# Passing from layer 1 to layer 2 one stream at a time, and new places for dense fill

## The chip, the core and the metric

One core of a Trainium2 chip. The kernel is one launch, and its time is the device time of that launch in microseconds (us). Five engines run their own instruction streams: PE (TensorE, the matmuls), DVE (VectorE), ACT (ScalarE), POOL (GpSimd) and SP (SyncE, which here only issues DMAs). A tile's data passes from one to the next by semaphores.

## What is computed

Two layers of a hybrid block over 256 latent tokens `x` and 256 context tokens `ctx`, width 1024. The reference, cut to the layer:

```python
for l in range(DEPTH):                       # DEPTH = 2
    mod_x = silu(c) @ w_mod[l] + b_mod[l]    # shift, scale, gate; the same for ctx with c_ctx
    hx  = rmsnorm(x,  g_pre[l]) * (1 + sc_x) + sh_x
    hcn = rmsnorm(hc, g_pre[l]) * (1 + sc_c) + sh_c
    # zx = hx @ w_in, zc = hcn @ w_in: cut into the three branches' inputs, their gates, merge gates
    o_rw, o_na, o_df = rwkv7_both_directions(z), neighbourhood_attention(z), differential_attention(z)
    yb = einsum('btnc,ncd->btnd', o * silu(g), w_branch)      # one 512 -> 1024 product a branch
    y  = sum(sigmoid(mg) * yb) @ w_out
    x  = x  + gt_x * rmsnorm(y_x, g_post[l])
    hc = hc + gt_c * rmsnorm(y_c, g_post[l])                  # not in the last layer
return x
```

The last layer needs the context only as keys, values and RWKV states, so its gates, merge and output product run for the 256 latent tokens alone.

## The kernel before

**Dense products.** Each float32 product is made of three products of rounded operands (`mm3`, L244: high·high, high·low, low·high). A weight comes in chunks of 128 × 512 (256 KB, `chunk`, L217, DMA issued by SP into a ring of 6 buffers `wr`); ACT rounds it to `wh` (ring of 5) and DVE subtracts to get the low part `wl` (ring of 4) (`split`, L226). The layer's input stands transposed in 16 tiles `self.h` (8 high, 8 low, features on the partitions, 512 tokens wide: columns 0 to 255 are x, 256 to 511 are ctx). `z_pair` (L270) makes 256 output features of it in four chunks.

**Order of the work.** The program is written as generators. The RWKV branch (`rwkv`: groups of scores, a triangular inverse `rwkv_inv` L777, state steps `rwkv_steps` L837, all in two segments) and then attention (`attn`, L1034) are the main strings. They yield numbers from the table `self.yl` (one row a layer), and `weave` (L1437) puts so much dense work (`fill`) between their pieces. Fill is, in this order, the projections and gates that the branches still need (`zs`, L1367: gates, `rwkv_z`, `mgates`, `attn_z`), beside it the gate part of the modulation (`mods`, L1361), and then the merge of branch 0 and 1. A bigger number in the table takes fill from later places, a smaller one leaves it to them; fill that is used up can't cover a wait. A list scheduler then settles each engine's order; each engine executes strictly in order.

**The passage.** After the third branch's merge, `merged` (L1261) adds and rounds the eight merged tiles `s`. `outproj` (L1269) multiplies all 512 tokens by `w_out`: 4 column groups `c` of 256, each of 4 chunks `kh`; a chunk serves 4 token tiles, so 24 matmuls of 256 columns. ACT squares and DVE multiplies by the gate row as each `c` ends. Then come, for all four token tiles at once, `residual` (L1299: reduce, `rsqrt` L201, 8 multiply-adds) and `start` (L449): `norm_rows`, the transposition of the rows by PE (`turn_rows`, 32 transposes of 128 × 128), the modulation by DVE and ACT and the split into `self.h`. The shift and scale of layer 2 (`mod_rows`, L362: 4 groups of 32 matmuls on 32 columns) run here too: the weights come during `outproj`, two of the groups run after its last matmul. Then follow r (chunk 0, x alone), the low-rank inputs (chunk 6), k and v.

**Tail.** In layer 2 `outproj` serves x's two token tiles, and `residual` writes the result.

The instruction helpers stand at L164 (ACT), L185 (tensor_tensor), L189 (tensor_scalar), L192 (scalar_tensor_tensor), L195 (matmul), L199 (transpose), L179 (reduce). In names, `k` is any general tile, `a`, `z`, `y`, `b` are PSUM tiles.

## Time and profile before

| | |
|---|---|
| median of 3 runs | 1435.5 us (1427.74 to 1436.76) |
| the profiled execution's own time | 1432.81 us |
| its span | 1430.8 us |
| mean granted clock of TensorE, share of full speed | 0.96 |
| PE busy | 1316.2 us (92%) |
| weight loads (PEld, beside PE) | 1099.1 us (77%) |
| DVE busy | 973.6 us (68%) |
| ACT busy | 812.4 us (57%) |
| POOL busy | 234.8 us (16%) |

So PE is the engine that sets the time, and 114.6 us of the span pass without a matmul. The stretches of the kernel, by the names on PE in the timeline: layer 1 up to 771.4 us, the passage 771.4 to 888.9, layer 2's first RWKV half to about 1134, its second inverse 1134.5 to 1193.4, second steps 1193.4 to 1236.8, attention 1252.5 to 1349, merges and output to the end.

### The profile page before, as it was taken

Reading aid. Unit: us, or ns where it says so; the run is one execution under the profiler, and the core shown is the slowest. Engines: PE = TensorE matmul, PEld = TensorE weight load, DVE = VectorE, ACT = ScalarE, POOL = GpSimd, SP = SyncE. Lnnn points to the kernel's source line nnn. Section 1 sums busy time; section 2 is a strip of 40 time slices with the busy share of each in tenths; the row PEclk is TensorE's granted clock in tenths of the full one; section 3 lists DMA queues with packets and bytes.
Section 4 is the critical chain, followed back from the end, with each engine's and each line's share of the span. In section 5 each row is a group of like instructions: output and inputs, shape, how many; then the busy total and the mean of one; then the engine's idle time right before and its main releaser. Section 6 shows DMA issues by size and latency. Waiting matters only on the chain. (4 is left out here: it accounts for less than half of the span.)

```text
span 1430.8 us, 28581 instructions
## 1 busy us (share of the span) xinstructions
PE 1316.2 (92%) x10784; PEld 1099.1 (77%) x10784; DVE 973.6 (68%) x2047; ACT 812.4 (57%) x1750; POOL 234.8 (16%) x292
## 2 busy tenths in 40 slices
PE   6999999999998999999899969998999998989796
PEld 4865877789777876677778948887888788967686
DVE  4763579626887367768675357768747892689886
ACT  5462375535864436667533356766549736477653
POOL 0010011002110011223245001011111000032441
PEclk9999999899998899999999989999989998999999
DMA  9366632414323268422643843553613242685454
GB/s 357 125 205 201 201 123 89 126 61 148 119 67 118 69 168 243 142 97 82 201 144 118 303 159 103 185 170 121 182 61 97 75 140 69 180 272 171 131 168 148
DMA packets 112986, 212.42 MB, mean 148 GB/s; under 512 B 13088, under 2 KB 24880, under 8 KB 112848
## 3 DMA queue, kind: packets, MB, share of 16 engines
q1 hardware_dynamic: 102896, 178.33, 39.3%
q0 software_dynamic: 9952, 32.26, 6.9%
q8 instruction: 85, 1.39, 0.4%
q14 instruction: 53, 0.43, 0.1%
HBM read 176.70 MB, written 33.83 MB: 147 GB/s over the span
## 5 line engine op out<-in xcount | busy, mean ns | idle before, releaser
L195 PE MATMUL z<-k,wh 128*128 128x512 f32 (+1 forms) x2288 | 631.7, 359 | 8.6 <-ACT wh L164 4.5
L195 PEld LDWEIGHTS z<-k,wh 128*128 128x128 f32 x2288 | 404.8, 193 | 75.1 <-issue 9.7
L195 PE MATMUL z<-k,wl 128*128 128x512 f32 (+1 forms) x1144 | 407.5, 358 | 8.5 <-DVE wl L185 8.5
L164 ACT ACTIVATE wh<-wr 128x512 fp32r<-128x512 f32 x376 | 234.0, 630 | 295.8 <-PE z L195 172.3
L185 DVE TENSOR_TENSOR wl<-wr,wh 128x512 fp32r<-128x512 f32 x376 | 280.3, 752 | 168.0 <-PE z L195 66.8
L195 PEld LDWEIGHTS z<-k,wl 128*128 128x128 f32 x1144 | 220.5, 193 | 41.5 <-DVE wl L185 13.0
L195 PE MATMUL z<-wh,k 128*128 128x256 f32 x704 | 142.1, 296 | 1.5 <-ACT k L164 1.3
L195 PEld LDWEIGHTS z<-wh,k 128*128 128x128 f32 x704 | 117.4, 201 | 3.4 <-ACT k L164 1.5
L185 POOL TENSOR_TENSOR k<-k,k 64x512 fp32r<-64x512 f32 (+3 forms) x64 | 78.4, 1231 | 165.9 <-ACT k L164 88.3
L195 PE MATMUL z<-wl,k 128*128 128x256 f32 x352 | 103.9, 295 | 1.7 <-DVE wl L185 1.5
L164 ACT ACTIVATE gs<-z 128x512 f32<-128x512 f32 (+1 forms) x132 | 66.2, 502 | 61.7 <-PE z L195 52.6
L164 ACT ACTIVATE k<-k 64x256 fp32r<-64x256 f32 (+5 forms) x154 | 79.2, 541 | 29.4 <-POOL k L185 21.6
L185 DVE TENSOR_TENSOR k<-k,k 128x256 f32<-128x256 f32 (+5 forms) x126 | 79.5, 644 | 17.5 <-ACT k L164 14.3
L199 PE MATMUL b<-cst,k 128*128 128x128 f32 x384 | 67.4, 292 | 20.7 <-ACT k L164 5.5
L199 PEld LDWEIGHTS b<-cst,k 128*128 128x128 f32 x384 | 45.3, 147 | 42.0 <-issue 13.6
L164 ACT ACTIVATE k<-a,s 128x512 f32<-128x512 f32 (+1 forms) x96 | 59.2, 617 | 32.1 <-DVE s L179 31.3
L164 ACT ACTIVATE k<-b 128x256 f32<-128x256 f32 (+1 forms) x152 | 67.4, 472 | 16.7 <-PE b L199 15.9
L195 PEld LDWEIGHTS z<-wl,k 128*128 128x128 f32 x352 | 70.8, 201 | 2.9 <-DVE wl L185 2.3
L195 PE MATMUL a<-k,k 128*128 128x512 f32 (+1 forms) x192 | 61.2, 400 | 12.1 <-ACT k L164 9.9
L195 PE MATMUL a<-ar,bk 64*128 64x128 f32 (+1 forms) x512 | 50.0, 285 | 9.8 <-ACT Lab L164 9.0
L195 PEld LDWEIGHTS a<-ar,bk 64*128 64x128 f32 x512 | 42.4, 187 | 21.5 <-ACT Lab L164 16.3
L179 DVE TENSOR_REDUCE s<-a 128x1 f32<-128x512 f32 (+1 forms) x96 | 56.4, 587 | 1.7 <-PE a L195 1.7
(169 smaller groups left out, 1952.4 us busy)
## 6 DMA issues: line engine op xcount, KB each, us to landing
wr<-in_wi SPq DMA_DIRECT2D x296, 256.0 KB, 3.0
k<-in_wm SPq DMA_DIRECT2D x64, 256.0 KB, 5.7
wr<-in_wb SPq DMA_DIRECT2D x48, 256.0 KB, 2.6
md<-gs SPq DMA_DIRECT2D x36, 256.0 KB, 2.8
k<-md POOLq DMA_DIRECT2D x36, 256.0 KB, 4.5
wr<-in_wg SPq DMA_DIRECT2D x32, 256.0 KB, 3.0
wr<-in_wo SPq DMA_DIRECT2D x32, 256.0 KB, 4.8
gd<-gs SPq DMA_DIRECT2D x18, 256.0 KB, 3.0
```

Of the source, the lines that this page charges most:

```text
L164: return self.nc.scalar.activation(out=out, in_=in_, func=func, **kw)
L179: return self.nc.vector.tensor_reduce(out=out, in_=in_, axis=AX.X, op=op, **kw)
L185: return (eng or self.nc.vector).tensor_tensor(out=out, in0=a, in1=b, op=op)
L195: return self.nc.tensor.matmul(out, lhsT=lhsT, rhs=rhs, start=start, stop=stop)
L199: return self.nc.tensor.transpose(out, in_, self.ident[0:k, 0:k])
```

## The change

1. `outproj` works on one stream, x first, then ctx, so `w_out` is read and split twice (16 chunks more). In the last column group the first token tile's four chunks run before the second tile's, and `done` (residual, `norm_row`) of the first tile follows at once. `stream_in` transposes, modulates and splits one stream, 256 columns wide. `start_next` then makes r and the RWKV gates of x, before chunks 6, 2 and 4, which need both streams.
2. While ctx's output product, r and these gates run, the low parts of the weights are made by POOL instead of DVE (`lo_eng`): 16 + 4 + 8 chunks.
3. The shift and scale of layer 2 (`mod_next`) are made in layer 1 as fill, one group after a piece of gates, through the ring `wr`.
4. The RWKV gates of layer 2 thereby leave its fill.
5. The table `yl` has new numbers, and `rwkv_inv` has two more places that take fill (`q`).
6. `rsqrt` for one column has 8 operations instead of 10. `residual` works by token tile, in the tail too. Two general slots fewer (50).

```diff
-        self.yl = [dict(inv=(59.8, 32.75), qq=(6, 9.66), step=(6, 6), na=(2.5, 1.19), diff=(0.8, 2.9), nd=(2, 5), A=(0, 0), B=(0, 4), G=(0.75, 0), C=(5.6, 7.2)),
-                   dict(inv=(25.5, 54), qq=(3.0, 0), step=(6, 6), na=(1.0, 2.3), diff=(4.69, 8.12), nd=(0, 2), A=(0, 0), B=(4.5, 0), G=(0, 0), C=(4.0, 6.0))]
+        self.lo_eng = None
+        self.yl = [dict(inv=(57, 30), qq=(6, 9.66), step=(6, 6), na=(2.5, 1.19), diff=(0.8, 2.9), q=(1.0, 1.0), nd=(2, 5), A=(0, 0), B=(0, 4), G=(0.75, 0), C=(5.6, 7.2)),
+                   dict(inv=(11.0, 51), qq=(4.5, 0), step=(6, 6), na=(1.0, 2.3), diff=(5.86, 8.12), q=(0, 1.0), nd=(3.0, 3.5), A=(0, 3.0), B=(4.5, 0), G=(0, 0), C=(0, 6.0))]
...
+        if n == 1:
+            a, y, t = (self.small(1) for _ in range(3))
+            self.ts(a, v, scale, eps, ALU.mult, op)
...
+            self.tt(y, t, y, ALU.mult)
+            return y
...
-        self.tt(lo, w, h.bitcast(F32), ALU.subtract)
+        self.tt(lo, w, h.bitcast(F32), ALU.subtract, self.lo_eng)
...
+    def mod_next(self, l, P):
+        rows = self.stage(512)
+        self.dma(self.nc.gpsimd, rows, self.io["rows"][l, :, 0:512])
+        A, B, gp = self.mod_tiles(l, P)
+        for g in range(4):
+            mp = self.ps("z", (128, 128))
+            for k in range(8):
+                w = self.chunk(self.io["wm"][l, g, k])
+                for i in range(4):
+                    self.mm(mp[32 * i:32 * i + 32, :], self.cs[:, k].rearrange("p a b -> p (a b)"),
+                            w[:, 128 * i:128 * i + 128], k == 0, k == 7)
+            self.mod_cols(A, B, gp, mp, rows[:, 128 * g:128 * g + 128], g)
+            yield 3.2
+            for _ in range(3):
+                yield 0
...
+    def stream_in(self, P, hn, s):
+        c = slice(256 * s, 256 * s + 256)
+        for k in range(8):
+            p = self.ps("b", (128, 256))
+            self.turn_rows(hn, k, p)
+            t = self.slot((128, 256))
+            A, B = P["A"][:, s, k:k + 1], P["B"][:, s, k:k + 1]
+            self.ts(t, p, A, B, ALU.mult, ALU.add)
+            self.act(self.h[0][k][:, c], p, AF.Identity, scale=A, bias=B)
+            self.tt(self.h[1][k][:, c], t, self.h[0][k][:, c].bitcast(F32), ALU.subtract)
+    def norm_row(self, x):
+        ss = self.small(2)
+        for j in range(2):
+            self.act(self.stage(512), x[j], AF.Square, accum_out=ss[:, j:j + 1])
+        s2 = self.small(1)
+        self.red(s2, ss, ALU.add)
+        rs = self.rsqrt(s2, 1, 1.0 / 1024, RMS_EPS)
+        self.act(x[0], x[0], AF.Copy, scale=rs)
+        self.ts(x[1], x[1], rs)
+    def start_next(self, l, P, nr):
+        self.lo_eng = self.nc.gpsimd
+        r = self.now(self.z_pair(l, 0, 0, nr))
+        self.rwkv_rows(l, P, 0, 1, r, 0, nr, False)
+        self.now(self.gates(l, nr, 0))
+        self.lo_eng = None
+        self.rwkv_wa(l, P, self.now(self.z_pair(l, 6, 0, T)), 0, T)
+        row = [self.rwkv_rows(l, P, 0, w, self.now(self.z_pair(l, c, 0, T)), 0, T, True) for w, c in ((0, 2), (2, 4))]
+        self.have["rx", l, 0] = True
+        self.have["rz", l, 0] = row[0], [None, None], row[1]
...
             Qs.append(q)
+            yield self.yl[e["l"]]["q"][e["sg"]]
...
+            if hf == 0:
+                yield self.yl[e["l"]]["q"][e["sg"]]
...
-    def outproj(self, l, s, ns, ss, ahead):
-        G = [self.gate_rows(l, st) for st in range(ns)]
-        y = []
-        for t in range(2 * ns):
+    def outproj(self, l, s, st, G, ahead, done):
+        y, ss = [], [self.small(4) for _ in range(2)]
+        for t in range(2):
             yt = self.k4.tile([128, 2, 512], F32, tag="k4", name=f"y{self.count()}")
             y.append([yt[:, 0, :], yt[:, 1, :]])
         for c in range(4):
-            p = [self.ps("za"[c % 2], (128, 2, 256)) for _ in range(ns)]
+            p = [self.ps("za"[c % 2], (128, 256)) for _ in range(2)]
+            cs = slice(256 * (c % 2), 256 * (c % 2) + 256)
+            def part(w, kh, t):
+                for k in range(2):
+                    kk = 2 * kh + k
+                    c0 = 256 * st + 128 * t
+                    self.mm3(p[t], [a[:, c0:c0 + 128] for a in s[kk]], [a[:, k, :] for a in w], kk == 0, kk == 7)
+            def read(t):
+                self.act(self.stage(256), p[t], AF.Square, accum_out=ss[t][:, c:c + 1])
+                self.tt(y[t][c // 2][:, cs], p[t], G[c // 2][:, cs], ALU.mult)
+            ws = []
             for kh in range(4):
-                w = self.split(self.io["wo"][l, c, kh])
+                ws.append(self.split(self.io["wo"][l, c, kh]))
                 ahead(4 * c + kh)
-                for t in range(2 * ns):
-                    for k in range(2):
-                        kk = 2 * kh + k
-                        self.mm3(p[t // 2][:, t % 2, :], [a[:, 128 * t:128 * t + 128] for a in s[kk]],
-                                 [a[:, k, :] for a in w], kk == 0 and t % 2 == 0, kk == 7 and t % 2 == 1)
-            cs = slice(256 * (c % 2), 256 * (c % 2) + 256)
-            for t in range(2 * ns):
-                pt = p[t // 2][:, t % 2, :]
-                self.act(self.stage(256), pt, AF.Square, accum_out=ss[:, 4 * t + c:4 * t + c + 1])
-                self.tt(y[t][c // 2][:, cs], pt, G[t // 2][c // 2][:, cs], ALU.mult)
-        return y
+                part(ws[kh], kh, 0)
+                if c < 3:
+                    part(ws[kh], kh, 1)
+            read(0)
+            if c == 3:
+                done(0, y[0], ss[0])
+                for kh in range(4):
+                    part(ws[kh], kh, 1)
+            read(1)
+        done(1, y[1], ss[1])
...
+    def residual(self, t, y, ss, xs, st, last):
+        s2 = self.small(1)
+        self.red(s2, ss, ALU.add)
+        rs = self.rsqrt(s2, 1, 1.0 / 1024, RMS_EPS)
+        for j in range(2):
+            rows = slice(128 * t, 128 * t + 128)
+            xo = xs[j]
+            self.stt(xo, y[j], rs, xo, ALU.mult, ALU.add)
...
                 def zs():
-                    yield from self.gates(l, nq, 0)
                     if l == 0:
+                        yield from self.gates(l, nq, 0)
...
-                    yield from self.gates(l, nq, 2)
-                    yield from self.mgates(l, nq, 1)
-                    yield from self.mgates(l, nq, 2)
+                    rest = self.chain(self.gates(l, nq, 2), self.mgates(l, nq, 1), self.mgates(l, nq, 2))
+                    yield from rest if last else self.both(self.mod_next(l + 1, PN), rest)
...
-                ss = self.small(8 if last else 16)
-                y = self.outproj(l, s, 1 if last else 2, ss, ahead)
+                    self.derived(l + 1, PN)
+                    self.h_new()
+                for st in range(1 if last else 2):
+                    xs = []
+                    def ahead(i):
+                        if i in (3, 7):
+                            self.rows_load(xsrc, 2 * st + i // 4, xs)
+                    def done(t, y, ss):
+                        self.residual(t, y, ss, xs[t], st, last)
+                        if not last:
+                            self.norm_row(xs[t])
+                    self.lo_eng = nc.gpsimd if st else None
+                    self.outproj(l, s, st, G[st], ahead, done)
+                    if not last:
+                        self.stream_in(PN, xs, st)
                 if not last:
-                    next(mod)
-                self.residual(y, ss, xs, last)
-                if not last:
-                    self.start(l + 1, PN, xs, mod, ws, NX)
+                    self.start_next(l + 1, PN, NX)
```

What the change does to the order of an engine, at three places.

**PE at the start of the output product of layer 1.** Each row is the first matmul of a run; `wh…` is a chunk of `w_out`, the `k` tile is the merged tile `s[2·kh]` or its low part, `z…` is the result. A chunk has 24 matmuls before and 12 after. Before:

```order
L195 MATMUL z1516_8573<-wh1518_8577,k1491_8528 128x256
...
L195 MATMUL z1516_8573<-wh1519_8607,k1495_8536 128x256
...
L195 MATMUL z1516_8573<-wh1520_8637,k1499_8544 128x256
...
L195 MATMUL z1516_8573<-wh1521_8667,k1503_8552 128x256
```

After:

```order
L197 MATMUL z1573_8831<-wh1575_8835,k1532_8756 128x256
...
L197 MATMUL z1573_8831<-wh1576_8853,k1536_8764 128x256
...
L197 MATMUL z1573_8831<-wh1577_8871,k1540_8772 128x256
...
L197 MATMUL z1573_8831<-wh1578_8889,k1544_8780 128x256
```

The fourth chunk, the first to need the last two merged tiles, stands behind 72 matmuls before and behind 36 after.

**PE behind the output product.** `y…` and the `z…` turned from `k1594` are the modulation, `b…` are the transposes of the normed rows. Before:

```order
L195 MATMUL a1575_9010<-wh1585_9109,k1506_8557 128x256
L195 MATMUL y1595_9157<-k1532_8719,cs_168 32x128 x4
...
L199 MATMUL z1655_9353<-cst_181,k1594_9155 128x128
...
L195 MATMUL y1595_9157<-k1602_9192,cs_168 32x128 x4
L199 MATMUL z1656_9400<-cst_181,k1594_9155 128x128
L199 MATMUL b1623_9252<-cst_181,k1522_8671 128x128
...
L199 MATMUL b1637_9301<-cst_181,k1587_9114 128x128
L195 MATMUL z1657_9406<-k1639_9308,wh1659_9410 128x512
```

After (`a1662`, `z1671` and `a1680` are ctx's output product, `z1725` is r, `z1732` the gates):

```order
L197 MATMUL a1662_9378<-wl1666_9436,k1546_8784 128x256
L201 MATMUL b1635_9247<-cst_181,k1579_8893 128x128
L201 MATMUL b1635_9247<-cst_181,k1589_8977 128x128
L197 MATMUL a1662_9378<-wh1666_9435,k1547_8785 128x256
L197 MATMUL z1671_9461<-wh1673_9465,k1532_8756 128x256
...
L197 MATMUL a1680_9542<-wh1684_9581,k1547_8785 128x256
L197 MATMUL z1725_9747<-k1553_8811,wh1727_9751 128x256
...
L201 MATMUL b1709_9691<-cst_181,k1657_9355 128x128
L201 MATMUL b1711_9698<-cst_181,k1657_9355 128x128
L197 MATMUL z1732_9829<-k1554_8812,wl1734_9834 128x256
```

Before, only modulation and transposes stand between the last matmul of the product and the first of the projections. After, x's transposes stand inside ctx's product, and ctx's inside x's r and gates.

**ACT in the second inverse of layer 2.** `Lab…` are the blocks of the inverse that PE's next product reads; `k…<-a…` are two intermediate copies that the last Lab blocks depend on, `wh…` are weight chunks. Before:

```order
L164 ACTIVATE Lab1980_12096<-X2174_13503 32x32x32 x2
L164 ACTIVATE Lab1980_12096<-X2175_13504 32x32x32
L164 ACTIVATE gs2169_1_13450<-z2163_13326 128x512
L164 ACTIVATE Lab1980_12096<-X2175_13504 32x32x32
L164 ACTIVATE wh2189_13785<-wr2189_13783 128x512
L164 ACTIVATE wh2198_13931<-wr2198_13929 128x512
L164 ACTIVATE wh2199_13943<-wr2199_13941 128x512
L164 ACTIVATE k2177_13540<-a2176_13507 32x512 x2
L164 ACTIVATE k2179_13576<-a2178_13543 32x512 x2
L164 ACTIVATE Lab1980_12096<-a2180_13583 32x16x32 x2
```

After:

```order
L166 ACTIVATE Lab1993_12064<-X2192_13487 32x32x32 x2
L166 ACTIVATE k2195_13524<-a2194_13491 32x512 x2
L166 ACTIVATE k2200_13590<-a2199_13557 32x512 x2
L166 ACTIVATE Lab1993_12064<-X2193_13488 32x32x32 x2
L166 ACTIVATE Lab1993_12064<-a2201_13597 32x16x32 x2
L166 ACTIVATE Lab1993_12064<-a2202_13632 32x16x32 x2
```

The copies `k` stand behind four Lab copies, a `gs` and three weight chunks before, and behind two Lab copies after.

## Rows read from the trace of the kernel before

**Rows 1.** Windows, passage: stretch, length, busy PE PEld DVE ACT POOL, clock, DMA, GB/s.

```profile
771.40:787.40 16.00, 13.92 (x99) 13.27 (x97) 8.60 (x14) 6.18 (x14) 8.20 (x8) 0.89 0.39 114
771.40:822.10 50.70, 48.62 (x390) 47.83 (x392) 21.35 (x39) 18.57 (x50) 8.20 (x8) 0.97 0.72 248
822.10:847.00 24.90, 12.53 (x164) 9.08 (x164) 16.73 (x64) 15.70 (x41) 2.73 (x5) 0.73 0.43 145
847.00:888.90 41.90, 41.90 (x314) 35.10 (x315) 26.71 (x62) 20.34 (x42) 1.65 (x3) 1.00 0.36 120
```

**Rows 2.** Windows view, layer 2: attention.

```profile
1252.50:1349.00 96.50, 83.95 (x535) 67.82 (x536) 83.96 (x176) 70.11 (x180) 33.22 (x39) 0.95 0.60 190
```

**Rows 3.** Windows view, layer 2: second inverse in two parts.

```profile
1134.50:1180.70 46.20, 44.20 (x281) 39.13 (x280) 42.72 (x88) 18.50 (x31) 3.77 (x4) 1.00 0.40 115
1180.70:1193.40 12.70, 8.28 (x273) 7.96 (x274) 1.29 (x2) 11.02 (x13) 0.00 (x0) 0.72 0.28 85
```

**Rows 4.** Windows view, layer 2: first and second state steps.

```profile
1040.80:1078.50 37.70, 37.65 (x494) 30.22 (x494) 17.12 (x32) 19.84 (x41) 5.14 (x4) 0.93 0.20 65
1193.40:1236.80 43.40, 43.40 (x760) 40.62 (x760) 18.56 (x26) 19.94 (x35) 4.63 (x3) 0.96 0.31 96
```

**Rows 5.** Timeline of the tail.

```profile
1420.47 0.28 PE L195 MATMUL a<-wh,k 128*128 128x256 f32 x1
...
1422.66 0.15 DVE L179 TENSOR_REDUCE s<-s 128x2 f32<-128x8 f32 x1
...
1424.62 2.74 DVE L192 SCALAR_TENSOR_TENSOR k<-y,s,k 128x512 f32<-128x512 f32 x4
```

**Rows 6.** Timeline of PE in the gap: start, duration, instruction and count.

```profile
824.95 1.95 PE L195 MATMUL y<-k,cs 128*32 128x128 f32 x64
...
840.53 5.12 PE L199 MATMUL b<-cst,k 128*128 128x128 f32 x24 [0.47 <-ACT k L164]
```

**Rows 7.** Windows view of the 24 transposes.

```profile
840.53:845.65 5.12, 5.12 (x24) 4.13 (x24) 2.83 (x8) 3.29 (x6) 0.00 (x0) 0.57 0.01 3
```

**Rows 8.** Windows view of stretches in which PE runs only dense matmuls.

```profile
787.40:798.90 11.50, 11.50 (x98) 11.50 (x97) 3.94 (x7) 2.74 (x7) 0.00 (x0) 1.00 1.00 350
875.97:884.13 8.16, 8.16 (x38) 6.76 (x36) 6.37 (x12) 6.12 (x13) 0.00 (x0) 1.00 0.32 94
```

**Rows 9.** Timeline of DVE, POOL and ACT for one merged tile.

```profile
779.73 0.68 DVE L192 SCALAR_TENSOR_TENSOR k<-k,a 128x512 f32<-128x512 f32 x1
780.56 1.59 POOL L185 TENSOR_TENSOR k<-k,k 128x512 f32<-128x512 f32 x1 [2.13 <-DVE k L192]
782.18 0.63 ACT L164 ACTIVATE k<-k 128x512 fp32r<-128x512 f32 x1 [2.56 <-POOL k L185]
782.84 0.69 DVE L192 SCALAR_TENSOR_TENSOR k<-k,k 128x512 fp32r<-128x512 f32 x1 [1.83 <-ACT k L164]
```

**Rows 10.** Groups by form: POOL's subtraction of that shape, over the whole run.

```profile
L185 POOL TENSOR_TENSOR k<-wr,k 128x512 fp32r<-128x512 f32 x16 | 21.4, 1346 | 33.2 <-ACT k L164 33.1
```

**Rows 11.** Timeline of POOL and DVE where both subtract or multiply at once.

```profile
748.01 1.31 POOL L185 TENSOR_TENSOR k<-k,k 128x512 f32<-128x512 f32 x1
748.72 1.42 DVE L185 TENSOR_TENSOR wl<-wr,wh 128x512 fp32r<-128x512 f32 x1 [0.73 <-PE z L195]
750.35 2.55 POOL L185 TENSOR_TENSOR k<-k,k 128x512 f32<-128x512 f32 x2
750.66 2.79 DVE L185 TENSOR_TENSOR wl<-wr,wh 128x512 fp32r<-128x512 f32 x1
```

**Rows 12.** Groups by form: the gate part of the modulation, already fed through `wr`.

```profile
L195 PE MATMUL y<-wr,cs 128*32 128x256 f32 x128 | 12.9, 401 | 1.9 <-DVE gt L185 1.4 <-DMA wr<-in_wg 0.5
```

**Rows 13.** Windows view, layer 1: end of attention and the third branch's merge.

```profile
696.20:735.00 38.80, 35.07 (x155) 27.95 (x156) 24.80 (x53) 14.93 (x32) 4.88 (x9) 0.96 0.45 155
```

**Rows 14.** Chain that ended last, second inverse: start, duration, engine, tile, line.

```profile
1177.90 2.08 ACT Lab L164
...
1189.55 5.74 PE a L195 x160
```

69 lines of the change are left out of this document (30 added, 39 removed).

## The prediction

> **What bounds the kernel now.** I read the granted clock first (0.96 over the span, so TensorE loses little to its clock outside single stretches), then the busy shares (PE 92%: the end comes earlier only where PE stops waiting), then PE's windows one after another, to find where the 114.6 us without a matmul lie, and there the timeline and the chain of waits, to see what is waited for. Four places bear on this change. In the passage PE is full while the output product runs, then has 12.5 us of work in a stretch of 24.9 us, then is full again [rows 1]. The beginning of the output product loses some: 16.0 us for its first column group [rows 1]. In layer 2, PE is without work 12.6 us of attention's 96.5 us [rows 2] and 4.4 us at the end of the second inverse [rows 3], while the state steps behind it are full [rows 4]. The tail after the last matmul is one chain on DVE [rows 5].
>
> What is moved between full stretches costs nothing by itself: PE runs the same number of matmuls of each shape before and after. So the sum is over waits that go and waits that come.
>
> **The gap after the output product.** It is 24.9 us [rows 1]. What PE does in it that is still to be done: two groups of modulation of 1.95 us each [rows 6], so 3.9 us, and 32 transposes. Of these 24 took 5.12 us at a granted clock of 0.57 [rows 6, 7], so 5.12 × 0.57 / 24 = 0.12 us each at the full clock, 3.9 us for 32. After the change they stand between matmuls, where the clock is full. 24.9 − 3.9 − 3.9 = 17.1: I take **−17**. It holds if PE has work while the second stream is normed. For x that is ctx's product: 192 matmuls × 0.12 us (11.5 us for 96 [rows 8]) = 23.0 us. For ctx it is r and x's gates: 48 + 96 matmuls × 0.12 = 17.3 us. What has to fit beneath it is a stream of two tiles, the first of which is normed early: half of the 24.9 us that four tiles took, 12.5 us. If no part went side by side it would be the whole 24.9 us, a wait of 7.6 us; that end goes into the next but one term.
>
> **The start of the output product: +5.** The eight merged tiles come one after another through DVE (0.68), POOL (1.59), ACT (0.63) and DVE (0.69) [rows 9], with 3.7 us from one to the next, and the order of these instructions doesn't change. The last one is ready at 782.84 + 0.69 = 783.5, when 72 matmuls of the first column group could run ahead of it; they wait anyway, and the group of 96 × 0.12 = 11.5 us ends at 787.4, 16.0 us after the merge, 4.5 us lost [rows 1]. After, only 36 matmuls (4.3 us) stand ahead of the same moment, 12 more follow (1.4 us and some clock), so the group of 48 (5.8 us) ends at about 785.5: 14.1 us for 5.8 us of work, 8.3 us lost, 3.8 more. PE waits longer there, and the clock of that stretch is already 0.89 [rows 1]; I add 1.2 us for it. Bounds +3 and +8.
>
> **POOL makes 28 low parts: +5.5.** PE's work from the start of ctx's product until x's gates end is 23.0 + 17.3 + 3.9 (transposes) = 44.2 us. POOL needs 1.35 us for such a subtraction [rows 10], 28 of them 37.7 us: less than 44.2, so POOL alone isn't the bound, but nearly. In the same stretch DVE must norm and modulate. Where both engines read two tiles from SBUF at once, DVE's 512-column subtraction took 1.42 us beside a POOL operation of 1.31, and 2.79 us beside two POOL operations of 2.55 together; both times DVE ended just after POOL [rows 11]. So they run one after the other: it is taken from DVE's side. DVE's own such operations are 8 multiply-adds of 0.69 (the 2.74 us for four in [rows 5]), 5.5 us, and 16 subtractions of 256 columns, at least half of 0.69 and at most 0.69 each, 5.5 to 11 us. In series with POOL: 48.7 to 54.2 us against 44.2, a wait of 4.5 to 10 us if all of it is serial, none if POOL's early start and its four buffers hide it. I take +5.5, nearer to the serial end because the row shows holds as long as the POOL operation.
>
> The Trainium skill says the same and speaks against this edit: by SBUF — State Buffer, section Who interferes with whom, a DVE instruction with two SBUF inputs contends with a GpSimd instruction that reads SBUF, and the one that comes second is held until the first has ended. By that rule the term would be the serial sum, up to +10; were there no such lock, 0. The trace agrees with the rule (1.42 and 2.79 us against 0.69).
>
> **Modulation and gates moved: −0.5.** The four groups (7.8 us) go from the passage into layer 1, where PE is the bound; neutral but for their 32 chunks through the ring of six. The gate part, with 32 chunks through the same ring, waited 1.9 us in all [rows 12], of which 0.5 for the DMA; I take +1.5 (0 to +6, if a group stood for a whole refill). The smaller inverse numbers leave more fill behind attention: 9.1 us of matmuls more than before come after it, and the end of attention with its merge had 3.7 us without a matmul in 38.8 [rows 13]: −2. The gates of layer 2 (11.5 us) go from fill to the passage; PE is the bound at both places.
>
> **Layer 2, attention: −6.5.** By the instruction order with 0.12 us for 256 columns and 0.227 us for 512 (8.16 / 36 [rows 8]), fill in attention grows from 31.7 to 43.3 us, +11.6. It finds 12.6 us without matmuls [rows 2]. But DVE is as busy there as PE (83.96 and 83.95 us), and each chunk of fill brings DVE a subtraction of some 0.7 us. Bounds −11.6 (all of it finds room) and 0 (DVE's chain sets the pace); the middle, a little to the better side, since the last units had no fill at all.
>
> **Layer 2, second inverse: −2.5.** DVE's part ends at 1177.9 [rows 14], PE's product waits until 1189.55 for ACT, which first makes Lab copies of about 2 us and weight chunks and only then the two copies `k` on which the last blocks depend. After the change the copies come earlier, and fill in the two inverse windows (58.9 us [rows 3]) falls by 6.9 us. My re-timing of ACT's part gives 49.1 us: −9.8, of which 6.9 is only work that went elsewhere, so −2.9 at best; +0.6 if the remaining fill doesn't cover the wait of 4.4 us. **The second steps: +2.3.** They lose 10.3 us of fill. They are 43.4 us and full; the nearest row, the first steps, took 37.7 us with 6 us more fill than is left here [rows 4]. If a chain sets a floor at 37.7, then 43.4 − 10.3 = 33.1 becomes 37.7, +4.6; if not, 0. I take half.
>
> **Tail: −2.7.** After the last matmul (1420.75) the reduce ends at 1422.81 and four multiply-adds at 1427.4 [rows 5]. The first tile's part is now done under the second tile's matmuls: two multiply-adds 1.37, one tile's reading 0.95, and 0.4 for two operations fewer (estimates from the same stretch). Bounds −3 and −1.4.
>
> **Sum:** −17 + 5 + 5.5 − 0.5 − 6.5 − 2.5 + 2.3 − 2.7 = −16.4. The profiled execution's 1432.8 becomes 1416.4. It lay 2.7 us below the median of the runs, 1435.5, on which the same step gives 1419.1.
>
> **Rivals.**
> *All is hidden.* POOL's and DVE's operations interleave (0 instead of +5.5), the start costs 3 instead of 5, attention takes in all its fill (−11.6): −16.4 − 5.5 − 2 − 5.1 = −29, about 1406.5. For it: POOL's sum is below PE's; against it: [rows 11], and DVE's share in attention.
> *Layer 2's new fill places buy nothing.* Attention 0, inverse +0.6, steps +4.6: −16.4 + 6.5 + 3.1 + 2.3 = −4.5, about 1431. For it: DVE equals PE in attention [rows 2], so more fill makes DVE's chain longer; against it: the idle time lies at the last units.
> *The shared port makes ctx's stretch DVE's (slower).* If each of POOL's subtractions holds DVE, DVE needs its own work, 16.7 us of the gap and 21.4 us of the product's stretch less the 16 low parts that POOL takes over (16 × 0.69 = 11.0) [rows 1], 27.1 us, plus 37.7 held, 64.8 against PE's 44.2: +20.6. PE then waits within each chunk, and its clock would fall as in the gap, to 0.57 [rows 7]: 44.2 / 0.57 − 44.2 = +33. With +27 between these the sum is −16.4 − 5.5 + 27 = +5.1, about 1440.6. It decides from a loss of 21.9 us in this stretch on. Against it: PE's order has r and the gates ready as work, and holds need overlap that the two engines don't always have.
> *The ring.* If the 32 modulation chunks stop the fill of layer 1 behind them, each group up to the 6 us of a refill, it is some +6: within the range.
>
> **Chances and range.** About 1% is what a measurement of this kernel can tell from no change: 1421.1 and 1449.9 are the bounds. The forecast (1411 to 1428) has 0.54, of which 0.33 lies below 1421.1. All hidden 0.14, faster. Fill buys nothing 0.20: 0.17 within 1%, 0.03 slower with mishaps of its kind. The port 0.12: 0.08 within, 0.04 slower. Together faster 0.47, same 0.46, slower 0.07. The range reaches halfway into the first rival, 1405, and over the second to 1436, leaving out about 0.07 below and 0.12 above. The forecast's own range is 1411 to 1428.
>
> **What would show it.** Right: PE's window between ctx's last product matmul and chunk 6 without a wait above 1 us and at a granted clock near 1; x's first column group about 14 us long; DVE's two-input operations lengthened to 1.4 us and more between ctx's product and the gates; fewer idle microseconds in layer 2's attention; the last matmul about 2.7 us nearer to the end. Wrong: waits for `wl` made by POOL on PE, a clock of 0.6 in that stretch, attention of layer 2 longer by the fill that it took in, or waits for `wr` in layer 1 where the modulation runs.

## Result: 1.4% slower, and where the time went

The changed kernel takes 1452.8 us (median of four runs, 1451.67 to 1459.52) against 1436.1 us: a ratio of 1.0136 over the runs, with a 95% interval of 1.0108 to 1.0163 (the two medians alone give 1.0116). The forecast was 1419.1 us with a range up to 1436. The profiled execution has a span of 1450.0 us against 1430.8, 19.2 us more where 16.4 us less were expected.

I cut both spans at the same places: at the first matmul of layer 1's output product and at the first score product of layer 2.

| stretch | before | after | difference | forecast |
|---|---|---|---|---|
| start to the output product | 771.6 | 798.5 | +26.9 | +7.3 (7.8 us of modulation moved in, −0.5) |
| passage, to layer 2's first scores | 139.0 | 147.3 | +8.3 | −2.8 (−7.8 and +11.5 moved, −17 +5 +5.5) |
| layer 2 | 520.2 | 504.2 | −16.0 | −20.9 (−11.5 moved, −6.5 −2.5 +2.3 −2.7) |
| span | 1430.8 | 1450.0 | +19.2 | −16.4 |

So 19.6 us of the miss lie in layer 1, 11.1 in the passage and 4.9 in layer 2. In layer 1 one stretch has most of it (15.4 us longer), from the end of its state steps to the last scores of attention. Windows view of the kernel before (stretch, length, busy time of PE, PEld, DVE, ACT, POOL, granted clock, DMA share, GB/s):

```profile
515.30:696.10 180.80, 171.60 (x884) 127.50 (x884) 143.08 (x326) 119.55 (x300) 48.04 (x45) 1.00 0.50 152
696.10:771.50 75.40, 71.57 (x316) 58.18 (x317) 50.52 (x83) 25.91 (x50) 28.63 (x32) 0.98 0.47 160
```

The same stretches of the changed kernel, then its output product, the two holes in the passage, and layer 2's attention, the end of its second inverse and its second steps:

```profile
520.70:716.90 196.20, 179.35 (x993) 130.06 (x994) 144.29 (x331) 119.60 (x302) 45.44 (x39) 0.96 0.53 164
716.90:798.50 81.60, 78.99 (x356) 63.76 (x356) 55.13 (x88) 29.89 (x57) 31.62 (x38) 1.00 0.52 173
...
798.50:868.00 69.50, 56.27 (x402) 54.35 (x401) 48.03 (x111) 35.87 (x86) 32.08 (x29) 0.85 0.55 173
...
835.00:842.00 7.00, 0.45 (x4) 0.43 (x3) 5.98 (x22) 3.54 (x10) 4.60 (x5) 0.74 0.60 210
875.00:881.00 6.00, 0.29 (x2) 0.29 (x3) 5.05 (x21) 3.21 (x9) 3.75 (x3) 0.86 0.38 104
...
1268.60:1366.00 97.40, 93.44 (x633) 78.39 (x634) 87.39 (x183) 73.40 (x187) 31.06 (x36) 0.98 0.63 196
1207.00:1218.10 11.10, 11.10 (x270) 10.51 (x270) 1.01 (x2) 10.30 (x12) 0.00 (x0) 0.50 0.17 52
1218.10:1252.50 34.40, 33.14 (x649) 29.40 (x649) 11.87 (x15) 13.45 (x23) 4.62 (x3) 0.96 0.23 70
```

The 24.9 us gap of [rows 1] is gone as one piece, but two new holes of 7.0 and 6.0 us stand in its place, one for each stream. Attention of layer 2 is PE's now: 4.0 us without a matmul in 97.4, where 12.6 in 96.5 were [rows 2]. What PE waited for in layer 1 stands in the view of waits (who waits for whom, 476 to 620 us: total us, times, longest), in the waits of SP's queue and in the timeline of that queue:

```profile
PE z L197 <- DMA wr<-in_wm: 5.3, 2, 3.3
```

```profile
SPq L169 <- DVE gs L194: 20.1, 2, 19.1
```

```profile
491.14 0.33 SPq L169 DMA_DIRECT2D wr<-in_wm  x1
510.59 0.33 SPq L169 DMA_DIRECT2D gd<-gs  x1
511.01 0.88 SPq L169 DMA_DIRECT2D wr<-in_wm  x2
```

SP issues six chunks of the second group (the last of them at 491.14), then holds for 19 us at the store of a gate, and the last two chunks come after it; PE is at the group by then and waits 2.0 us. From there on the loads of modulation, of attention and of the next weights come in one burst: 25.8 MB between 476 and 600 us, where the kernel before moved 20.6. The waits for the chunks themselves are only 5.3 us; what else the loads cost is measured below.

In the passage PE's waits are those of the transposes for the normed rows (first line) and, at the start of the output product, those for low parts of `w_out` (second line):

```profile
PE b L201 <- ACT k L166: 15.7, 5, 6.5
PE z L197 <- DVE wl L187: 3.2, 2, 2.0
```

And DVE's timeline shows what the norm itself waits for. These are operations on one number per partition, in the chain of the inverse square root, the first while POOL makes low parts, the second just after:

```profile
836.75 2.98 DVE L194 SCALAR_TENSOR_TENSOR s<-s,s 128x1 f32<-128x1 f32 x1
839.65 0.14 DVE L181 TENSOR_REDUCE s<-s 128x1 f32<-128x4 f32 x1
839.76 0.16 DVE L194 SCALAR_TENSOR_TENSOR s<-s 128x1 f32<-128x1 f32 x1
```

```profile
836.00 3.71 POOL L187 TENSOR_TENSOR wl<-wr,wh 128x512 fp32r<-128x512 f32 x3
```

An operation of 0.16 us takes 2.98 us, and ends with POOL's three subtractions of some 1.25 us each: it was held beyond the end of one of them.

### The profile page after: what moved, and what is told of

Same layout as the page of the kernel before. It is cut to its first block, busy times and chain, and to the rows that moved or that the text cites. A ratio compares the mean times of both kernels' runs of the same rounds, so it can differ in the third digit from the quotient of the medians.

```text
span 1450.0 us, 28779 instructions
## 1 busy us (share of the span) xinstructions
PE 1326.3 (91%) x10784; PEld 1104.5 (76%) x10784; DVE 995.5 (69%) x2089; ACT 816.6 (56%) x1766; POOL 271.0 (19%) x320
## 5 line engine op out<-in xcount | busy, mean ns | idle before, releaser
L197 PE MATMUL z<-k,wh 128*128 128x512 f32 (+1 forms) x2352 | 652.5, 361 | 8.2 <-ACT wh L166 4.2
L197 PEld LDWEIGHTS z<-k,wh 128*128 128x128 f32 x2352 | 417.9, 194 | 75.9 <-issue 9.2
L197 PE MATMUL z<-k,wl 128*128 128x512 f32 (+1 forms) x1176 | 420.2, 359 | 11.5 <-DVE wl L187 11.4
L166 ACT ACTIVATE wh<-wr 128x512 fp32r<-128x512 f32 x392 | 242.8, 630 | 272.6 <-PE z L197 156.6
L187 DVE TENSOR_TENSOR wl<-wr,wh 128x512 fp32r<-128x512 f32 x364 | 274.6, 762 | 157.8 <-PE z L197 67.4
L197 PEld LDWEIGHTS z<-k,wl 128*128 128x128 f32 x1176 | 227.0, 194 | 47.0 <-DVE wl L187 17.3
L197 PE MATMUL z<-wh,k 128*128 128x256 f32 x704 | 148.4, 302 | 1.6 <-ACT k L166 1.0
L201 PE MATMUL b<-cst,k 128*128 128x128 f32 x384 | 68.5, 289 | 33.5 <-ACT k L166 16.4
L187 DVE TENSOR_TENSOR k<-k,k 128x256 fp32r<-128x256 f32 (+5 forms) x134 | 80.7, 613 | 16.9 <-ACT k L166 13.4
L166 ACT ACTIVATE k<-b 128x256 f32<-128x256 f32 (+1 forms) x144 | 62.8, 465 | 27.6 <-PE b L201 26.9
L187 DVE TENSOR_TENSOR ht<-a,H 128x512 f32<-128x512 f32 x12 | 8.3, 692 | 72.4 <-PE a L197 72.4
L197 PEld LDWEIGHTS a<-ar,bk 64*128 64x128 f32 x512 | 42.1, 187 | 20.7 <-ACT Lab L166 15.2
```

The source lines that it names most:

```text
L166: return self.nc.scalar.activation(out=out, in_=in_, func=func, **kw)
L187: return (eng or self.nc.vector).tensor_tensor(out=out, in0=a, in1=b, op=op)
L197: return self.nc.tensor.matmul(out, lhsT=lhsT, rhs=rhs, start=start, stop=stop)
L201: return self.nc.tensor.transpose(out, in_, self.ident[0:k, 0:k])
```

## Experiments

Lengths of the three stretches, from each kernel's profiled execution, and the ratio to the kernel before as measured beside it. Kernels whose instructions on PE are the same, in the same order, up to the end of layer 1's state steps reached that point between 520.7 and 526.5 us, so 6 us in the first column say nothing. The passage repeats within 1 us where nothing was changed, layer 2 within 4 us: in the ten changed kernels with 50 slots, whose matmuls there stand in the same order, it takes 502.3 to 506.0 us.

| kernel | to output product | passage | layer 2 | ratio (95%) |
|---|---|---|---|---|
| before | 771.6 | 139.0 | 520.2 | |
| changed | 798.5 | 147.3 | 504.2 | 1.0136 (1.0108 to 1.0163) |
| four modulation loads | 782.5 | 148.2 | 503.8 | 1.0006 (0.9982 to 1.0030) |
| one-input inverse root | 804.3 | 143.1 | 506.0 | 1.0147 (1.0120 to 1.0175) |
| low parts on DVE | 805.1 | 138.4 | 503.2 | 1.0070 (1.0045 to 1.0096) |
| table row of layer 1 as before | 802.6 | 147.6 | 505.1 | 1.0141 (1.0112 to 1.0169) |
| modulation in the merges | 809.9 | 147.3 | 503.8 | 1.0175 (1.0151 to 1.0199) |
| the same, low parts on DVE | 811.7 | 137.6 | 503.0 | 1.0095 (1.0060 to 1.0130) |
| one input, x stored by SP | 804.2 | 142.8 | 504.8 | 1.0125 (1.0099 to 1.0150) |
| modulation in slots, DVE | 791.7 | 128.8 | 502.3 | 0.9923 (0.9902 to 0.9943) |
| the same, ctx turned later | 790.5 | 127.4 | 504.2 | 0.9927 (0.9908 to 0.9947) |
| changed, 52 slots | 806.0 | 147.5 | 499.5 | 1.0098 (1.0071 to 1.0125) |
| before, 50 slots | 771.1 | 139.2 | 518.8 | 0.9963 (0.9946 to 0.9981) |
| best | 781.1 | 135.7 | 498.8 | 0.9885 (0.9846 to 0.9924) |

### Layer 1: the modulation's loads

```diff
             for k in range(8):
-                w = self.chunk(self.io["wm"][l, g, k])
+                if k == 0:
+                    w = self.chunk(self.io["wm"][l, g, k])
```

> The changed kernel, but the modulation of layer 2 that is made in layer 1 reads one weight chunk for each of its four groups instead of eight: 28 of 32 loads are left out, all matmuls stay (so the modulation's values are not those wanted). Theory 1: layer 1 became 27 us longer, of which 7.8 us are the moved matmuls and some 18 us are SP's queue and the ring of six weight buffers, in which the 28 loads stand ahead of the weights, gate stores and bias tiles of attention's start. Then the time falls by 13 to 19 us, to about 1437, and the window from the state steps to attention's second quarter loses its 16 us without matmuls. Theory 2: the new numbers of the table and the order of fill cost those 18 us. Then the time stays within 4 us of 1453.

Measured: 1434.8 us, 18 us faster than the changed kernel. Its stretch from the state steps to the last scores (windows view) has a length of 181.8 us, 14.4 less, with the same 993 recorded matmuls in it:

```profile
519.10:700.90 181.80, 173.77 (x993) 128.14 (x994) 141.43 (x329) 118.26 (x299) 45.59 (x39) 0.99 0.49 147
```

Theory 1 holds: 16.0 of the 19.6 us in layer 1 go with the 28 loads. Of the 14.4 us in this stretch, 8.8 are time without a matmul (16.9 us in the changed kernel, 8.0 here), and 5.6 are the same matmuls taking less time (179.35 us at a granted clock of 0.96, 173.77 at 0.99). The passage and layer 2 stay as they were. This shows that the loads cost it, and leaves open whether by the ring, by SP's queue or by the bytes.

The rival, layer 1's new row of the table:

```diff
-        self.yl = [dict(inv=(57, 30), ..., q=(1.0, 1.0), ...
+        self.yl = [dict(inv=(59.8, 32.75), ..., q=(0, 0), ...
```

> The changed kernel with layer 1's row of the table as before the change (59.8 and 32.75 for the inverses, no fill at the two new places). Theory 1 (the modulation's loads cost layer 1 its 18 us): no more than 4 us either way, 1449 to 1457. Theory 2 (the table costs it): 10 us faster or more.

Measured: 1455.5 us, no different. Layer 1's row of the table is not the cause.

Then the place. The four groups go beside the merges of the first two branches, through the same ring (with one empty step behind a group instead of three):

```diff
-                    yield from rest if last else self.both(self.mod_next(l + 1, PN), rest)
+                    yield from rest
...
+                merges = self.chain(self.merge(l, 0, acc, nq), self.merge(l, 1, acc, nq))
+                fill = self.chain(self.both(mods(), zs()), merges if last else self.both(merges, self.mod_next(l + 1, PN)))
```

> The changed kernel with the four modulation groups woven into the merges of the first two branches (one group after every second piece of merge) instead of the gates and projections ahead of attention. The same 32 loads through the same ring and queue. Theory 1 (it is the place: at attention's start the loads stand in SP's queue ahead of what attention waits for, and DMA is full there): the time falls by 10 to 18 us, to 1435 to 1443, and no wait for in_wm above 2 us is left. Theory 2 (8.4 MB through a ring of six cost their transfer time wherever they stand): 1448 or more.

Measured: 1462.4 us. Attention's stretch is healed (180.7 us, as before), and the work behind it, until the output product, took up more than was won: 112.1 us instead of 81.6, of which only 7.8 are the modulation's matmuls:

```profile
697.80:809.90 112.10, 94.74 (x578) 72.31 (x578) 51.59 (x99) 28.81 (x62) 34.41 (x42) 0.85 0.58 196
```

PE is without a matmul for 17.4 us of it, where the changed kernel had 2.6, and the granted clock is 0.85 instead of 1.00. Most of the idle time is waiting for the modulation's chunks (who waits for whom in this stretch):

```profile
PE z L197 <- DMA wr<-in_wm: 12.0, 6, 4.4
```

So the place alone was not the cause, and the time is the one of theory 2: a group of eight chunks gives PE 1.95 us of work, and at both places it waits for its chunks. Whether it is the depth of the ring or the bytes, two kernels were to tell. One loads the modulation by POOL's queue into a ring of its own, taken from the general slots; the other makes the ring eight deep:

```diff
-                w = self.chunk(self.io["wm"][l, g, k])
+                w = self.wm.tile([128, 512], F32, tag="wm", name=f"wm{self.n}")
+                self.dma(self.nc.gpsimd, w, self.io["wm"][l, g, k].rearrange("p a b -> p (a b)"))
...
-NSLOT = 50
+NSLOT = 46
```

> The changed kernel with the 32 modulation chunks at their old place in the program, but loaded by POOL's queue into a ring of four of their own (four general slots fewer); SP's queue and the ring of weights are free of them, the bytes are the same. Theory 1 (SP's queue and the shared ring hold up what stands behind): 10 to 18 us faster than the changed kernel, 1435 to 1443. Theory 2 (the DMA engines are full there, share 1.05, so the bytes cost): less than 5 us faster. Theory 3: POOL, which also loads gates, is held by waiting for its ring, and attention's gate loads come late: slower.

```diff
-            self.wr, self.wh, self.wl = pool("wr", 6), pool("wh", 5), pool("wl", 4)
+            self.wr, self.wh, self.wl = pool("wr", 8), pool("wh", 5), pool("wl", 4)
...
-NSLOT = 50
+NSLOT = 48
```

> The changed kernel with a ring of eight weight buffers instead of six (two general slots fewer). Theory 1 (depth of the ring): a whole group of eight chunks can be loaded ahead, and layer 1 is 6 to 14 us shorter: 1439 to 1447. Theory 2 (the loads in SP's queue ahead of attention's own, or the full DMA, whatever the ring): within 4 us of 1453.

Measured: 1725.6 and 1632.0 us. They say nothing on the question: in both, the scheduler took layer 1's fill earlier (the modulation's matmuls begin at 374 and 386 us instead of 480), and its inverses ran uncovered (the first state steps begin at 586 and 536 us instead of 295). Whether the other rings or the slots given up for them brought this about was not tried. What settles it in part is a kernel in which the bytes stay and the loads run further ahead, up to 16 chunks in general slots, as in the kernel before, with the groups beside the third merge (and the low parts on DVE, below):

```diff
-                self.now(self.merge(l, 2, acc, nq))
+                m2 = self.merge(l, 2, acc, nq)
+                self.now(m2 if last else self.both(m2, self.mod_next(l + 1, PN)))
...
+        ws = []
+        self.mod_load(l, ws, 8)
         for g in range(4):
+            self.mod_load(l, ws, 8 * g + 16)
+            yield 0
...
-                w = self.chunk(self.io["wm"][l, g, k])
+                w = ws[8 * g + k]
```

> The low parts on DVE, and the modulation of layer 2 beside the third merge, its chunks loaded into general slots (up to 16 ahead) instead of the ring of six, as the kernel before does in the output product. Theory 1 (a group of 8 chunks gives PE only 1.95 us of work and the ring holds 6, so each group waits for its transfers unless they were made ahead): the loads no longer stop anything, layer 1 loses only the 7.8 us of matmuls, and the time is that of the DVE kernel (1445.6) less 13 to 18: 1428 to 1433. Theory 2 (8.4 MB more in layer 1 cost their transfer time wherever they stand): above 1440.

Measured: 1424.5 us, 21 us below the kernel with low parts on DVE and the ring, and below the kernel before. The 8.4 MB are still in layer 1, and no matmul of the modulation waits for a chunk any more, so it is not the bytes as such. But the gain is not all the loads'. By the profiled executions the kernel is 23.9 us shorter than the one with low parts on DVE and the ring: 9.3 us up to the end of layer 1's state steps, where groups and waits for chunks stood, 4.1 from there to the output product, 0.9 in layer 2, and 9.6 in the passage, whose code is the same. The last group now stands just ahead of the product, where PE had waited for the last merged tiles, and the first column group takes 5.8 us instead of 13.2 (windows view, the changed kernel and this one):

```profile
798.50:811.70 13.20, 9.05 (x49) 7.96 (x48) 9.38 (x22) 5.09 (x11) 7.62 (x7) 0.72 0.29 83
791.70:797.50 5.80, 5.80 (x50) 5.80 (x50) 2.42 (x6) 2.72 (x7) 0.00 (x0) 1.00 1.03 374
```

So this kernel changes the place as well as how far ahead the chunks are asked for; the place, the depth of the ring and SP's queue were not separated.

### The passage: POOL and the small operations

```diff
     def start_next(self, l, P, nr):
-        self.lo_eng = self.nc.gpsimd
...
-                    self.lo_eng = nc.gpsimd if st else None
```

> The changed kernel with all 28 low parts made by DVE again, as before the change. Theory 1 (the shared port): DVE is held no longer, each small operation takes 0.2 us; DVE has 28 x 0.7 = 20 us more of its own, beside PE's 44 us. The two waits of over 6 us for transposes shrink to 2 or 3 us and the time falls by 5 to 10 us. Theory 2 (DVE's own load): DVE becomes the bound in ctx's stretch, chunks wait for their low parts, and the time stays or rises by up to 5 us.

Measured: 1445.6 us, and the passage is 8.9 us shorter, 138.4 us; the output product took 57.7 us instead of 69.6 and the rest 3.0 us more. DVE's operations on one column between 826 and 900 us, by form (busy us, mean ns), first in the changed kernel:

```profile
L194 DVE SCALAR_TENSOR_TENSOR s<-s,s 128x1 f32<-128x1 f32 x24 | 15.4, 648 | 0.3
L194 DVE SCALAR_TENSOR_TENSOR s<-s 128x1 f32<-128x1 f32 x8 | 5.5, 684 | 0.1
```

and with the low parts on DVE:

```profile
L194 DVE SCALAR_TENSOR_TENSOR s<-s,s 128x1 f32<-128x1 f32 x24 | 4.5, 195 | 0.1
L194 DVE SCALAR_TENSOR_TENSOR s<-s 128x1 f32<-128x1 f32 x8 | 1.2, 153 | 0.0
```

32 operations cost 20.9 us beside POOL and 5.7 us without, 15.2 us less, in the chains of the norms that PE's transposes wait for; that DVE makes 28 subtractions more (28 × 0.69 = 19 us) cost less than that. Theory 1 has the time. Of its waits, those for x's norm in the product fell from 9.0 us to 0.7; that in ctx's half did not go (6.2 us in the changed kernel, 4.7 and 3.4 here, below). The second form reads the same tile twice and is held as well.

Then the same with POOL at work, but the small operations in a form with one tensor input:

```diff
-            self.stt(t, y, a, y, ALU.mult, ALU.mult)
+            self.ts(t, y, a, y, ALU.mult, ALU.mult)
```

(and so for the other four).

> The changed kernel, but the inverse square root of one column is written with tensor_scalar operations alone, both scalars read per partition, so that no operation of it has two tensor inputs; the same eight operations and values. Theory 1: in the passage its 128x1 operations wait behind POOL's 1.28 us subtractions (0.16 us alone, 1.2 to 3 us beside POOL); eight norms, some 2 to 4 us each where POOL works. Then these operations take 0.2 us, the four chains of ctx and x shorten by 3 us each or more, PE's waits for the transposes (6.6, 2.5, 6.2 us) fall to half, and the time falls by 5 to 9 us, to about 1446. Theory 2: the waits come from the place at which the transposes stand in PE's order, and another 1 us of chain makes no difference: within 3 us of 1453.

Measured: the passage is 4.2 us shorter (143.1), the time is not (1456.3 us; in its profiled execution 5.8 us more lie ahead of anything that was edited). The operations do go free, 242 ns instead of 648:

```profile
L191 DVE TENSOR_SCALAR s<-s,s 128x1 f32<-128x1 f32 x32 | 7.7, 242 | 0.9
```

but the passage gains a third of the some 13 us that this takes off DVE, since the next thing is late: the scaling of a row in place waits for that row's store, which POOL issues behind its subtractions.

```profile
845.51 0.49 DVE L191 TENSOR_SCALAR k<-k,s 128x512 f32<-128x512 f32 x1 [3.31 <-DMA xd<-k]
```

So the store went to SP:

```diff
-                self.dma(self.nc.gpsimd, self.xd[rows, 512 * j:512 * j + 512], xo)
+                self.dma(self.nc.sync, self.xd[rows, 512 * j:512 * j + 512], xo)
```

> The one-input inverse square root with POOL still making the 28 low parts, and the store of x (xd) issued by SP instead of POOL. Theory 1: with the small operations freed, the in-place scaling of a row waited up to 3.3 us for the store that stands behind subtractions in POOL's queue; now this wait goes too and the stretch from the output product's start to the first score product of layer 2 is 3 to 6 us shorter than in the one-input kernel (143.1 us), below 140. Theory 2: the chain isn't what PE waits for: the stretch stays within 1.5 us of 143.

Measured: 142.8 us in the passage, as theory 2 has it, and 1455.0 in all. The wait for the store fell to 0.64 us, and the scaling itself was held in its turn, like the big operations around it (the multiply-adds took 1048 ns on average where the changed kernel had 749, the 256-column subtractions 757 instead of 545):

```profile
842.60 1.30 DVE L191 TENSOR_SCALAR k<-k,s 128x512 f32<-128x512 f32 x1 [0.64 <-DMA xd<-k]
```

0.49 us free, 1.30 beside POOL. Each thing that was freed met the next hold; of what was tried, only taking POOL's subtractions away ended it. So the small operations by themselves are 4 of the 8.9 us.

Both at once, the modulation in the merges and the low parts on DVE (the two edits above):

> The modulation in the merges and all low parts on DVE, else the changed kernel. If the two losses are independent, the gain is the sum of the two single ones: 1453 less 10 to 18 for the place of the modulation less 7 for DVE, so 1428 to 1436; if the passage merely passes on a delay, one of them alone.

Measured: 1450.3 us, 12 less than with the modulation in the merges alone. The sum's first part failed (above). The second adds up: POOL's low parts cost the passage 9.7 us here and 8.9 with the modulation at its other place, so that loss does not hang on where the modulation stands.

### What is left of the gap

With the low parts on DVE, PE still waits in ctx's half (who waits for whom, 862 to 900 us):

```profile
PE b L201 <- ACT k L166: 4.7, 1, 4.7
PE z L197 <- DVE s L194: 3.4, 1, 3.4
```

r and the gates are 144 matmuls. The trace of the changed kernel has 53 of them ahead of ctx's first transposes (6.6 us), this kernel's 72. The next kernel's has 102, 30 more (the text below has the same 30, counted from 55):

```diff
-        self.now(self.gates(l, nr, 0))
+        g = self.gates(l, nr, 0)
+        for _ in range(4):
+            next(g)
+        self.now(self.both(g, stream))
```

(and the first transpose is kept in program order).

> The kernel with modulation in slots and low parts on DVE, and in addition ctx's transposes placed later in PE's order: 85 matmuls (10.2 us) of r and the gates ahead of the first one instead of 55 (6.6 us). Theory 1 (the order, not the work available, leaves PE waiting for ctx's norm, 4.7 and 3.4 us in the DVE kernel): 2 to 5 us less in the stretch from the output product's end to layer 2's first scores. Theory 2 (the norm's chain itself with the modulation of eight tiles behind it is longer than r and the gates): the wait only moves behind the gates, within 1.5 us.

Measured: the stretch from the product's end to the first scores went from 80.5 to 78.4 us, the low end of theory 1, but the time did not fall (1425.1 us), and the two waits have become one:

```profile
PE z L197 <- DVE s L194: 7.6, 1, 7.6
```

PE stops at 848.9 us. The gates need the PSUM tiles that r fills and DVE reads, and DVE's reading of r stands behind the norm's operations (DVE's timeline, the end of the second tile's multiply-adds and the first reading of r):

```profile
852.63 1.41 DVE L194 SCALAR_TENSOR_TENSOR k<-y,s,k 128x512 f32<-128x512 f32 x2
...
855.35 0.47 DVE L194 SCALAR_TENSOR_TENSOR gs<-z,pc,gs 128x255 f32<-128x255 f32 x1
```

So PE can't run further ahead, and the wait only moves, as theory 2 has it, but for another reason (read from the trace, not tried by itself).

### Slots, and a better kernel

The slots first, in the changed kernel and, the other way round, in the kernel before:

```diff
-NSLOT = 50
+NSLOT = 52
```

> The changed kernel with 52 general slots instead of 50, as before the change. With a ring of eight and 48 slots the kernel took 180 us longer, so slots may be scarce. Theory 1 (the loss is the modulation's loads and POOL's subtractions): within 4 us of 1453. Theory 2 (the two slots taken away hold up loads, in layer 1 above all): 6 us faster or more, and the waits for in_wm in layer 1 shrink.

> The kernel before with 50 general slots instead of 52. Theory 1: within 5 us of the kernel before. Theory 2 (two slots are worth something by themselves): 6 us slower or more, in the output product above all, where up to 24 modulation chunks stand in slots beside 16 merged tiles.

Measured: 1452.3 us and 1432.2 us. The two slots cost nothing in layer 1 or the passage; the kernel before is 0.4% faster with 50. In layer 2 of the changed kernel they do count: with 52 slots PE's matmuls stand in another order there, and the layer takes 499.5 us, below all the kernels with 50. The time without a matmul is the same (42.2 and 42.7 us); the same 4362 matmuls take 5.2 us less. Layer 2 of the changed kernel, of the one with 52 slots and of the best kernel below, whose matmuls there stand in the order of the second:

```profile
945.80:1450.00 504.20, 462.01 (x4362) 412.54 (x4361) 377.90 (x785) 311.58 (x679) 89.71 (x111) 0.95 0.46 143
953.50:1453.00 499.50, 456.82 (x4362) 405.74 (x4361) 378.00 (x785) 312.35 (x679) 90.50 (x111) 0.96 0.47 144
916.80:1415.60 498.80, 455.42 (x4362) 404.70 (x4361) 378.25 (x785) 312.16 (x679) 90.61 (x111) 0.97 0.47 144
```

The ratios, 1.0098 against 1.0136, point the same way, though their intervals overlap.

The best kernel has the low parts on DVE, the modulation in slots with two groups beside the third merge and two within x's output product, ctx turned later, and 52 slots:

```diff
+                for i, _ in enumerate(m2):
+                    if i in (1, 3):
+                        next(mod, None)
...
+                        if st == 0 and i in (4, 9):
+                            next(mod, None)
```

> An attempt at a better kernel: low parts on DVE, modulation through general slots, two groups beside the third merge and two within x's output product, ctx's transposes later, 52 slots. If the transfers that stand before the first chunks of w_out cost the third merge its 4 us (PE waited 3.1 us for the first chunk in the kernel with later transposes) and the start of the output product can use a modulation group as work, 3 to 7 us faster than that kernel (1425): 1418 to 1422. If the 8 MB in front of w_out simply delay it, it stays at 1425 or above.

Measured: 1419.1 us, a ratio of 0.9885 (0.9846 to 0.9924): it beats both kernels. Output product and what follows (windows view):

```profile
781.10:837.20 56.10, 54.31 (x529) 52.91 (x530) 41.11 (x123) 32.30 (x84) 3.59 (x6) 0.97 0.65 208
837.20:916.80 79.60, 70.85 (x387) 60.64 (x385) 58.67 (x143) 49.19 (x106) 7.38 (x12) 0.94 0.47 142
```

PE is without a matmul for 1.8 us in the product, with two modulation groups as work in it, where the changed kernel had 13.2 and the one with the modulation in slots 0.4. Its 8.7 us after the product are the wait above.

The forecast number came, but not from where it was looked for. By the profiled executions the best kernel is 6.5 us shorter than the one with ctx turned later. 5.4 of that lie in layer 2, where only the slots reach, and 3.2 ahead of the end of layer 1's state steps, which is within what equal programs differ by. From there to layer 2's first scores, where the modulation was moved, it takes 402.2 us against 400.1. So the move of two groups into the product bought nothing that shows; the slots in the kernel with ctx turned later, and nothing else, were not tried.

## Why the prediction was wrong, step by step

**Modulation and gates moved: −0.5.** This is the step that failed most: +19.6. I took the gate part, 32 chunks through the same ring at 1.9 us of waits [rows 12], as the like case. There each chunk had 0.40 us of PE (12.9 us over 32), here 0.24 (7.8 over 32), and its groups were spread between other work, mostly two chunks at a time, while each group here wants eight chunks in 1.95 us from a ring of six. The bound, "+6, if a group stood for a whole refill", counted one refill for four groups. Worked out per group it would have been 4 × 4 us (an estimate: eight chunks of 256 KB at the 350 GB/s of [rows 8] are 6 us, less 1.95 of work). I also looked at the waits for the chunks only: the changed kernel waited 5.3 us for them, and removing 28 loads gave back 16. The rest is what came late with them, and 5.6 us of matmuls at a lower granted clock, for which the prediction has no term.

**POOL makes 28 low parts: +5.5.** The bounds held (8.9 us, by taking it back, against 0 to 10), but I had priced only the large operations. What I left out are the 32 operations on a single column: held by POOL they made 20.9 us instead of 5.7, and freeing them alone gave back 4 of the 8.9. The Trainium skill's rule (SBUF — State Buffer, Who interferes with whom) covers them: it speaks of two SBUF inputs and of whole instructions, not of sizes. The trace agrees, and goes further: one that takes 0.16 us took 2.98, until the end of a run of three of POOL's instructions and not of one.

**The gap: −17.** Of the two holes that remain, the one in ctx's product was POOL's: with the low parts on DVE PE waits 0.7 us for x's norm there, not 9.0. The one behind the product shows the condition that I named, "if PE has work while the second stream is normed", and had counted but not looked up: 17.3 us of work existed, and 6.6 us of it stood ahead of the transposes in PE's order, which was to be had. Putting more of it ahead only moved the wait, since the gates themselves wait for DVE behind the norm. With the port's cost taken away the passage is 138.4 us, where the prediction without that term gives 130.7 (139.0 − 7.8 + 11.5 − 17 + 5); 8.1 us are the two waits of ctx's half.

**The start: +5.** The first column group took 13.2 us for 5.8 us of matmuls, where 14.1 and more were expected; before it was 15.8 for 11.5. That is 3.1 more lost, the lower bound. Two of the waits there (3.2 us) are put down to low parts of `w_out`, which DVE makes between the operations on the merged tiles, and only the third (1.0 us) to a merged tile, of which alone the prediction speaks. Where a modulation group stands just ahead of the product, as in the kernel with slots, nothing is lost here.

**Layer 2.** Attention took in 11.6 us more fill and became 0.9 us longer (97.4 against 96.5 [rows 2]): −10.7, near the better bound, where I took −6.5. DVE, as busy as PE before, did not set the pace. The second steps took 34.4 us against the 35.4 expected. At the second inverse the 4.4 us wait of [rows 3] is gone, and yet from the last scores to its end 50.9 us follow instead of 57.4: 6.5 less for 6.9 us of moved work, so nothing gained instead of −2.5; the wait now stands ahead of that (5.2 us without a matmul between 1165 and 1207 us, where before 2.0 lay between 1136 and 1180.7). The tail became 1.8 us shorter, not 2.7, because the first tile's two multiply-adds stand across the end of the matmuls and hold up the second tile's reading (the last matmul ends at 1441.76; DVE's timeline):

```profile
1441.67 1.42 DVE L194 SCALAR_TENSOR_TENSOR k<-y,s,k 128x512 f32<-128x512 f32 x2
1443.01 0.42 DVE L187 TENSOR_TENSOR y<-a,k 128x256 f32<-128x256 f32 x1
...
1445.18 1.41 DVE L194 SCALAR_TENSOR_TENSOR k<-y,s,k 128x512 f32<-128x512 f32 x2
```

These add up to some 6 us more than layer 2 gained in all (−16.0 with the 11.5 of the gates). They went to places that the prediction has no term for. Counted by PE's matmuls at 0.12 and 0.227 us, the dense work ahead of the second segment's scores fell by 6.8 us and not by the 11.5 of the gates, so other fill came in there (that stretch is 5.6 us shorter, 167.3 against 172.9), and 2.6 us more stand behind attention's last scores.

**The rivals.** The one that came true was the one given the least room, the ring, "some +6: within the range", and its sign, waits for `wr` in layer 1 where the modulation runs, is the one that showed. Whether it is the ring or the queue before it stays open. The slower rival named the right port and overpriced it: 9 us, not 27, and PE's clock in the product stretch was 0.85, not 0.57.

## What to carry to other kernels

When work that reads much and computes little is moved into fill, price its loads and not its matmuls: bytes per microsecond of work against the depth of the ring that they pass through, for each group, and what stands behind them in the issuing queue. Before counting work as cover, count how much of it stands ahead of the waiting instruction in the engine's order, and whether that work waits for the same chain. And when a second engine is given DVE's large operations, look at DVE's smallest ones, in chains: here each could be held for a whole instruction of the other, and one for more than two. And when a variant gains, see in which stretch: the best kernel's last gain lies in layer 2, far from the edit that it was meant to test.

## Of the hardware, not expected

A 128 × 1 operation of DVE with two tensor inputs, also with the same tile twice, took 0.65 to 0.68 us on average and up to 2.98 beside POOL's subtractions of some 1.25 us, 0.15 to 0.20 us without them. A tensor_scalar of 128 × 512 from SBUF to SBUF, with one tensor input, took 0.49 us and was seen at 1.30 beside POOL. And the same instructions of PE in the same order reached the end of layer 1's state steps anywhere between 520.7 and 526.5 us in different kernels, so a single profile does not resolve 5 us there.
